# PSUM pools per kind of tile, square sums behind the last blocks, and a source-ordered load queue between the up and down projections

## The chip, the cores and the metric

The kernel runs on one NeuronCore of one Trainium2 chip. The metric is the device time of one execution in microseconds (us); times are medians over executions of the same kernel.

## What is computed

A bidirectional encoder trunk over a sequence of 1024 tokens of width 1024, float32 throughout: an mLSTM layer and a windowed attention layer, each followed by a SwiGLU feed-forward network (FFN) of inner width 2816, and a final RMSNorm. The change touches what surrounds the FFNs.

```python
def rmsnorm(x, w):
    y = x * lax.rsqrt(jnp.mean(x * x, axis=-1, keepdims=True) + EPS)
    return y * w

def swiglu(h, w_in, w_out):
    gu = h @ w_in                                  # 1024 x (2 * 2816)
    gate, up = gu[..., :D_FF], gu[..., D_FF:]
    return (jax.nn.silu(gate) * up) @ w_out

def reference(x, ...):
    for i in range(2):
        hn = rmsnorm(x, norm_mix_w[i])
        x = x + (mlstm_mixer(hn, ...) if i == 0 else window_attn_mixer(hn, ...))
        x = x + swiglu(rmsnorm(x, norm_ffn_w[i]), ffn_w_in[i], ffn_w_out[i])
    return rmsnorm(x, norm_final_w)
```

## The kernel before

**Layout.** Everything is feature-major: x is eight blocks of 128 features by 1024 tokens, `self.x[0..7]`, and each block has two halves of 512 tokens (one PSUM bank holds 128x512 float32). A float32 product is made of three matmuls on parts: each operand is split into a high part (a copy to the narrower type on ScalarE, ACT) and a low part (a subtraction on VectorE, DVE, or on GpSimd, POOL). L200/L201 are the two halves of that split for hidden blocks and for the left operands of the up projection, L187/L188 (ACT, POOL) for the weights of the down projection (`wh`, `wl`). Buffers of 128x1024 come from one shared SBUF pool (`unit`), whether they hold weights as loaded (`raw`), hidden blocks (`hraw`, `hh`, `hl`), blocks of x, or rotary tables (`slab`). Weights are fetched two tiles ahead (`feed`, AHEAD = 2) by SyncE (SP).

**End of a mixer.** `out_pair` multiplies by the output weights block by block; `done` adds each half to x (DVE, L684). In the FFN's mixer, after each pair of blocks (i, i + 4), it also makes the *forms*, the right operands of a Strassen-like product of seven (`norm_forms`: f, f23, f12, f34), squares both blocks (ACT, L291), adds the squares to R (DVE, L292) and stores both blocks to DRAM (`keep_x`, ACT's queue, L243).

**Up projection.** `ffn_up` goes over 22 blocks of 128 hidden features; for each, `seven` (L524) runs seven products into five PSUM accumulators pa, pe, pb, pc, pd, and ACT, DVE and POOL make silu(gate) * up of them. In the first block all five accumulators begin with the first three forms, and the last form comes later. RMSNorm's scale isn't applied to the forms but to the accumulators (`R0`, `R1`): the sums of R over features are 16 matmuls of one column (L357), DVE and POOL make 1/sqrt of them (L345 to L350), two *spreads* (L368, 8 small matmuls each) bring that back to all partitions, and ACT copies them to R (L372). Each finished hidden block goes to DRAM (`hkeep`, L590, ACT's queue).

**Down projection.** `ffn_down` goes over three chunks of hidden blocks (0 to 5, 6 to 13, 14 to 21) and, inside each, over the eight output blocks d; a d of the first chunk is 2 halves of 18 matmuls (L620). Before it, hidden blocks are read back and split (`hidden`), and all of x is read back in 16 halves (`load_x`, L240). Behind each d it adds the product to x (DVE, L647), reads one hidden block of the next chunk, and in the first FFN runs three steps of `rope_tables` (DVE, lines 1107 to 1146), whose positions are loaded by SP (L1109).

**What sets the order.** A compile-time scheduler decides the order of instructions on each engine; each engine then runs its list strictly in order. SP and ACT each have one list in which DMA issues stand with the rest, so an issue that has to wait holds back what follows. DMA completions are counted on eight counters in rotation, and a DMA waits for the one that used its counter before it. `phase` opens the SBUF and the PSUM pool of a stage; in it, tags share the pool, and the next phase's pool takes over banks when the old pool is given back. The banks per tag are mm=2, pn=2, pk=2, mx=2 in the mLSTM phase, mm=3, sc=2, tp=2, mx=1 in the attention phase, and mm=6, mx=2 in the FFN phases.

## Time and profile before

| | us |
|---|---|
| median of 3 executions | 2319.24 (2316.86 to 2319.30) |
| the profiled execution | 2319.65 |
| its span, first to last instruction | 2317.9 |
| tensor engine (PE) busy | 2222.8 (96%) |
| VectorE (DVE) busy | 1403.9 (61%) |
| ScalarE (ACT) busy | 839.3 (36%) |
| GpSimd (POOL) busy | 593.8 (26%) |

The up projections lie at about 510 to 950 and 1605 to 2050 us of the span, each followed by its down projection. In the timelines a row is a start, a duration (or that of several instructions, then with a count) and, in brackets, how long the engine stood before it and what released it. PEclk is the clock that the tensor engine was granted, as a share of 2.4 GHz; 0.5 is its lower level of 1.2 GHz.

### The profile page before, as it was taken

How to read it: one execution, taken by the hardware profiler on the slowest of the kernel's cores; microseconds unless marked ns; L12 is line 12 of the kernel's file. 1: busy time of each engine (PE TensorE's matmuls, PEld its weight loads, DVE VectorE, ACT ScalarE, POOL GpSimd, SP SyncE). 2: the span in 40 equal slices, each digit the busy share in tenths (PEclk: the TensorE clock that was granted, in tenths of full speed). 3: DMA queues.
4: the chain of work that ended last, by engine and by line, in shares of the span. 5: the costliest groups of instructions: out<-in, count | busy, mean ns of one | idle time of the engine just before them, and what ended most of it. 6: DMA issues, size and time to landing. Idle time of an engine off the chain costs nothing.

```text
span 2317.9 us, 28270 instructions
## 1 busy us (share of the span) xinstructions
PE 2222.8 (96%) x10713; PEld 1825.4 (79%) x10713; DVE 1403.9 (61%) x2526; ACT 839.3 (36%) x1544; POOL 593.8 (26%) x398
## 2 busy tenths in 40 slices
PE   7899999989999999999999899898999999999998
PEld 4789898767888888788878777686788888878888
DVE  6355675787666666692224689779866666643112
ACT  4334444343222222321222578665322222232021
POOL 2212213312111111231333455540211111123143
PEclk9999999999999999999999999899999999999999
DMA  3111104222222221632323344503222222263112
GB/s 131 41 37 47 60 24 141 85 108 86 82 82 82 82 82 66 225 127 64 101 73 110 115 144 138 185 16 112 74 81 82 82 82 82 76 242 118 47 54 73
DMA packets 75959, 216.75 MB, mean 94 GB/s; under 512 B 8320, under 2 KB 14976, under 8 KB 75824
## 3 DMA queue, kind: packets, MB, share of 16 engines
q1 hardware_dynamic: 64216, 177.07, 23.6%
q10 hardware_dynamic: 11608, 37.89, 4.1%
q8 instruction: 84, 1.38, 0.2%
q14 instruction: 51, 0.42, 0.1%
HBM read 159.15 MB, written 55.77 MB: 93 GB/s over the span
## 4 chain that ended last, share of the span: by engine, by line
PE 78%; DVE 9%; issue 4%; DMA 3%; POOL 3%; ACT 2%; SPq 0%; POOLq 0%; DVEq 0%; ACTq 0%
PE mm L524 36%; PE mm L620 17%; PE mm L228 14%; PE mm L468 4%; PE pn L212 2%; PE mx L1307 1%; PE tp L1292 1%; PE sc L1263 1%; DMA slab<-bounce 1%; PE pk L212 1%; DMA raw<-in_a_in_dram 1%; DVE slab L1133 1%; DMA slab<-ykeep 1%; DVE e L1268 1%; POOL wl L188 1%
## 5 line engine op out<-in xcount | busy, mean ns | idle before, releaser
L188 POOL TENSOR_TENSOR wl<-raw,wh 128x1024 fp32r<-128x1024 f32 (+2 forms) x96 | 232.8, 2430 | 616.9 <-ACT wh L187 401.7
L620 PE MATMUL mm<-hh,wh 128*128 128x512 f32 (+1 forms) x768 | 289.2, 379 | 7.8 <-ACT wh L187 4.6
L620 PE MATMUL mm<-hh,wl 128*128 128x512 f32 (+1 forms) x768 | 290.4, 378 | 2.1 <-POOL wl L188 2.1
L620 PE MATMUL mm<-hl,wh 128*128 128x512 f32 (+1 forms) x768 | 290.3, 378 | 1.1 <-DVE hl L201 1.1
L571 POOL TENSOR_TENSOR t<-t,R 128x512 f32<-128x512 f32 x44 | 58.6, 1333 | 590.6 <-ACT t L570 590.6
L620 PEld LDWEIGHTS mm<-hh,wh 128*128 128x128 f32 x768 | 145.4, 190 | 37.8 <-ACT wh L187 5.5
L620 PEld LDWEIGHTS mm<-hh,wl 128*128 128x128 f32 x768 | 145.6, 190 | 31.7 <-POOL wl L188 3.3
L620 PEld LDWEIGHTS mm<-hl,wh 128*128 128x128 f32 x768 | 145.6, 190 | 30.8 <-DVE hl L201 2.4
L647 DVE TENSOR_TENSOR x<-x,mm 128x512 f32<-128x512 f32 x80 | 54.7, 685 | 181.6 <-PE mm L620 179.8
L228 PE MATMUL mm<-slab,wh 128*128 128x512 f32 x512 | 152.0, 404 | 5.5 <-ACT wh L187 1.9
L570 ACT ACTIVATE t<-t 128x512 f32<-128x512 f32 x44 | 27.8, 632 | 327.7 <-DVE t L569 327.7
L524 PE MATMUL mm<-f12h,wbl 128*128 128x512 f32 x352 | 138.6, 395 | 0.9 <-DVE wbl L201 0.9
L524 PE MATMUL mm<-f12h,wbh 128*128 128x512 f32 x352 | 138.8, 394 | 0.0
L524 PE MATMUL mm<-f12l,wbh 128*128 128x512 f32 x352 | 138.6, 394 | 0.0
L187 ACT ACTIVATE wh<-raw 128x1024 fp32r<-128x1024 f32 (+3 forms) x106 | 102.0, 969 | 75.0 <-DVE hl L201 57.9
L228 PE MATMUL mm<-hnh,wh 128*128 128x512 f32 x416 | 126.2, 403 | 0.9 <-DVE x L647 0.9
L562 DVE TENSOR_TENSOR t<-mm,t 128x512 f32<-128x512 f32 x44 | 30.4, 692 | 157.0 <-PE mm L524 157.0
L228 PE MATMUL mm<-hnh,wl 128*128 128x512 f32 x416 | 124.4, 400 | 0.4 <-POOL wl L188 0.4
L228 PE MATMUL mm<-hnl,wh 128*128 128x512 f32 x416 | 124.1, 400 | 0.0
L524 PE MATMUL mm<-f,wah 128*128 128x512 f32 x352 | 113.1, 403 | 11.1 <-DVE x L684 11.1
L524 PE MATMUL mm<-f34h,wd 128*128 128x512 f32 x352 | 117.6, 394 | 0.0
L1280 POOL TENSOR_TENSOR e<-e,smd 128x768 f32<-128x768 f32 (+1 forms) x64 | 89.3, 1397 | 101.7 <-DVE smd L1279 62.4
(291 smaller groups left out, 5292.0 us busy)
## 6 DMA issues: line engine op xcount, KB each, us to landing
raw<-in_ffn_in_dram SPq DMA_DIRECT2D x88, 512.0 KB
hkeep<-hs ACTq DMA_DIRECT2D x44, 512.0 KB
hraw<-hkeep SPq DMA_DIRECT2D x44, 512.0 KB
raw<-in_ffn_out_dram SPq DMA_DIRECT2D x32, 512.0 KB
raw<-in_m_in_dram SPq DMA_DIRECT2D x24, 512.0 KB
xkeep<-x ACTq DMA_DIRECT2D x24, 512.0 KB
x<-xkeep SPq DMA_DIRECT2D x48, 256.0 KB
bounce<-slab SPq DMA_DIRECT2D x40, 256.0 KB
```

The lines of the kernel that those rows point to most:

```text
L187: nc.scalar.activation(hi[:, c], r[:, c], AF.Copy)
L188: (nc.vector if fast else nc.gpsimd).tensor_tensor(lo[:, c], r[:, c], hi[:, c].bitcast(F32), op=ALU.subtract)
L212: self.nc.tensor.matmul(out, lhsT=l, rhs=r, start=start and i == 0, stop=stop and i == len(jobs) - 1,)
L228: self.nc.tensor.matmul(st["ps"], lhsT=l, rhs=r, start=j == 0, stop=j == len(jobs) - 1)
L468: self.nc.tensor.matmul(st[c], lhsT=l, rhs=r, start=j == 0 and a == 0, stop=j == 1 and a == len(jobs) - 1)
L524: self.nc.tensor.matmul(ps, lhsT=l, rhs=r, start=start and j == 0, stop=stop and j == len(jobs) - 1, skip_group_check=True,)
L562: V.tensor_tensor(u2, pb, p1, op=ALU.add)
L570: A.activation(g0, g0, AF.Silu)
L571: G.tensor_tensor(g0, g0, R0, op=ALU.mult)
L620: nc.tensor.matmul(po, lhsT=l, rhs=r, start=j == 0, stop=j == len(jobs) - 1)
L647: V.tensor_tensor(x, x, po, op=ALU.add)
L1280: G.tensor_tensor(e[:, j:j + 2, :n], e[:, j:j + 2, :n], d.unsqueeze(2).broadcast_to([P, 2, n]), op=ALU.mult,)
```

## The change

1. `phase` opens one PSUM pool per tag instead of one for all, so that a bank is given back with its own tag's pool; the FFN phases name mx before mm, so mx takes the first two banks and mm the six behind.
2. In `out_pair`, the squares, the adds to R and `keep_x` of blocks 2 and 6 no longer come between the third and fourth forms but behind the fourth, with those of 3 and 7.
3. From the last block of the up projection to the end of chunk 0 of the down projection, SP takes its instructions in source order (`manual_schedule`, closed behind d = 7). The weight split `ahead()` and hidden blocks 0; 1 and 2; 3; 4 are spread over the last up block, and the last `hkeep` store is issued behind the last of their hh splits (`issue_after`).
4. x is read back in full blocks (`fetch_x`, one load of 128x1024 each): two ahead of the loop and block d + 2 behind d.

The diff, cut to its core:

```diff
...
@@ -104,10 +104,12 @@
     @contextmanager
     def phase(self, name, n_t2, banks, spare=False):
         tc = self.tc
-        with tc.tile_pool(name=name, bufs=2) as tmp:
-            with tc.tile_pool(name=name + "p", bufs=2, space=PSUM) as ps:
-                self.tmp, self.n_t2, self.ps, self.banks, self.spare = tmp, n_t2, ps, banks, spare
-                yield
+        with tc.tile_pool(name=name, bufs=2) as tmp, ExitStack() as es:
+            ps = {
+                tag: es.enter_context(tc.tile_pool(name=name + tag, bufs=n, space=PSUM)) for tag, n in banks.items()
+            }
+            self.tmp, self.n_t2, self.ps, self.banks, self.spare = tmp, n_t2, ps, banks, spare
+            yield
 
     def unit(self, dtype=F32, name="slab"):
         return self.sl.tile([P, UNIT], dtype, name=self.nm(name), tag="unit")[:, :S]
@@ -122,7 +124,7 @@
         return self.t([P, HALF], dtype, "t2", self.n_t2)
 
     def bank(self, tag):
-        return self.ps.tile([P, HALF], F32, name=self.nm(tag), tag=tag, bufs=self.banks[tag])
+        return self.ps[tag].tile([P, HALF], F32, name=self.nm(tag), tag=tag, bufs=self.banks[tag])
 
     def setup(self):
         nc, c = self.nc, self.const
@@ -238,6 +240,11 @@
             o = slice(half * HALF, (half + 1) * HALF)
             for d in range(KT):
                 self.nc.sync.dma_start(self.x[d][:, o], src[:, d, o])
+
+    def fetch_x(self, d):
+        if d < KT:
+            self.x.append(self.unit(name="x"))
+            self.nc.sync.dma_start(self.x[d], self.xkeep[:, d])
 
     def keep_x(self, d):
         self.nc.scalar.dma_start(self.xkeep[:, d, :], self.x[d])
@@ -527,14 +534,18 @@
 
     def ffn_up(self, i):
         nc = self.nc
+        self.order = ExitStack()
         V, A, G = nc.vector, nc.scalar, nc.gpsimd
         cur, self.first = self.first, None
         self.hs = {}
         for f in range(NF):
+            if f + 1 == NF:
+                self.order.enter_context(self.tc.manual_schedule(engines={mybir.EngineType.SP}))
             if f + 1 < NF:
                 nxt, todo = self.left()
             else:
-                nxt, todo = None, [self.ahead] + [lambda k=k: self.hidden(i, k) for k in range(3)]
+                nxt, todo = None, [lambda k=k: self.hidden(i, *k) for k in ((0,), (1, 2), (3,), (4,))]
+                self.ahead()
             more = lambda: todo.pop(0)() if todo else None
             hs = self.unit(name="hs")
             R0, R1 = self.Rv(0), self.Rv(1)
@@ -587,14 +598,17 @@
             V.tensor_tensor(u3, pd, u3, op=ALU.add)
             V.tensor_tensor(hs[:, :HALF], g0, u3, op=ALU.mult)
             more()
-            nc.scalar.dma_start(self.hkeep[i][f], hs)
+            with self.tc.issue_after(self.hi.ins) if nxt is None else nullcontext():
+                nc.scalar.dma_start(self.hkeep[i][f], hs)
             cur = nxt
 
-    def hidden(self, i, f):
-        raw = self.unit(name="hraw")
-        self.nc.sync.dma_start(raw, self.hkeep[i][f])
-        self.hs[f] = self.unit(F32R, "hh"), self.unit(F32R, "hl")
-        self.split(*self.hs[f], raw)
+    def hidden(self, i, *fs):
+        for f in fs:
+            raw = self.unit(name="hraw")
+            self.nc.sync.dma_start(raw, self.hkeep[i][f])
+            hi, lo = self.hs[f] = self.unit(F32R, "hh"), self.unit(F32R, "hl")
+            self.hi = self.nc.scalar.activation(hi, raw, AF.Copy)
+            self.nc.vector.tensor_tensor(lo, raw, hi.bitcast(F32), op=ALU.subtract)
 
     def ffn_down(self, i, which, final=False, spill=None, side=()):
         nc = self.nc
@@ -604,7 +618,9 @@
         for f in range(len(hs), FF_CHUNKS[0][1]):
             self.hidden(i, f)
         self.ahead()
-        self.load_x(self.xkeep)
+        self.x = []
+        for d in range(2):
+            self.fetch_x(d)
         for ci, (f0, f1) in enumerate(FF_CHUNKS):
             last = ci == len(FF_CHUNKS) - 1
             if last:
@@ -647,11 +663,15 @@
                     V.tensor_tensor(x, x, po, op=ALU.add)
                     if last:
                         self.norm_add(d, half)
+                if ci == 0:
+                    self.fetch_x(d + 2)
                 if ahead:
                     self.hidden(i, ahead.pop(0))
                 if ci < 2:
                     for _ in range(3):
                         next(side, None)
+                if (ci, d) == (0, KT - 1):
+                    self.order.close()
                 if last and spill is not None:
                     self.keep_x(d)
         self.norm_end()
@@ -689,9 +709,10 @@
                         for f in todo:
                             f()
                     self.norm_forms(i)
-                    for k in (i, i + 4):
-                        self.norm_square_row(k)
-                        self.keep_x(k)
+                    for j in ((0,), (1,), (), (2, 3))[i]:
+                        for k in (j, j + 4):
+                            self.norm_square_row(k)
+                            self.keep_x(k)
 
             return self.product(pairs, done, 6)
 
@@ -1405,12 +1426,12 @@
     def run(self):
         self.setup()
         self.mlstm()
-        with self.phase("f0", 9, dict(mm=6, mx=2), True):
+        with self.phase("f0", 9, dict(mx=2, mm=6), True):
             self.attn_setup()
             self.ffn_up(0)
             self.ffn_down(0, 2, spill=self.xkeep, side=self.rope_tables())
         self.attn()
-        with self.phase("f1", 9, dict(mm=6, mx=2), True):
+        with self.phase("f1", 9, dict(mx=2, mm=6), True):
             self.ffn_up(1)
             self.ffn_down(1, 4, final=True)
 
```

Three places in the listing of instructions show it. On SP, between the up and the down projection of the first FFN, before (the rows begin with the last of the 16 loads of x, which follow hkeep 5, the last hidden block of chunk 0; hkeep 6 is the first of chunk 1):

```order
L240 DMA x_8193<-xkeep 128x512
L168 DMA raw_8229<-in_ffn_out_dram 128x768
L595 DMA hraw_8256<-hkeep_6_75 128x1024
L1109 DMA slab_8266<-in_pos_dram 128x1024
L168 DMA raw_8293<-in_ffn_out_dram 128x768
L595 DMA hraw_8320<-hkeep_7_76 128x1024
L168 DMA raw_8348<-in_ffn_out_dram 128x768
L595 DMA hraw_8375<-hkeep_8_77 128x1024
```

The same place after the change (lines have moved: L595 is now L608, L168 now L170, L1109 now L1130, and L247 is `fetch_x`):

```order
L608 DMA hraw_8197<-hkeep_5_74 128x1024
L247 DMA x_8203<-xkeep 128x1024
L247 DMA x_8205<-xkeep 128x1024
L170 DMA raw_8226<-in_ffn_out_dram 128x768
L247 DMA x_8253<-xkeep 128x1024
L608 DMA hraw_8255<-hkeep_6_75 128x1024
L1128 DMA invf<-in_invf_dram 128x1
L1130 DMA slab_8265<-in_pos_dram 128x1024
L170 DMA raw_8292<-in_ffn_out_dram 128x768
L247 DMA x_8319<-xkeep 128x1024
```

The load of hkeep 6 stood behind all of x, and now stands behind three blocks of it and ahead of the positions.

On ACT, around the last store of the up projection (hkeep 21), before:

```order
L200 ACTIVATE hh_8119<-hraw_8117 128x1024
L570 ACTIVATE t_1391_8109<-t_1391_8109 128x512
L574 ACTIVATE t_1389_8093<-t_1389_8093 128x512
L590 DMA hkeep_21_90<-hs_8033 128x1024
L200 ACTIVATE hh_8142<-hraw_8140 128x1024
L200 ACTIVATE hh_8163<-hraw_8161 128x1024
L200 ACTIVATE hh_8170<-hraw_8168 128x1024
L200 ACTIVATE hh_8176<-hraw_8174 128x1024
L200 ACTIVATE hh_8182<-hraw_8180 128x1024
L187 ACTIVATE wh_8231<-raw_7899 128x768
L200 ACTIVATE hh_8258<-hraw_8256 128x1024
L187 ACTIVATE wh_8295<-raw_8062 128x768
```

and after (L590 is now L602, the hh splits L610, the wh splits L189, the silus L581 and L585):

```order
L610 ACTIVATE hh_8087<-hraw_8085 128x1024
L610 ACTIVATE hh_8142<-hraw_8140 128x1024
L581 ACTIVATE t_1394_8132<-t_1394_8132 128x512
L610 ACTIVATE hh_8148<-hraw_8146 128x1024
L585 ACTIVATE t_1392_8116<-t_1392_8116 128x512
L610 ACTIVATE hh_8171<-hraw_8169 128x1024
L610 ACTIVATE hh_8192<-hraw_8190 128x1024
L602 DMA hkeep_21_90<-hs_8056 128x1024
L610 ACTIVATE hh_8199<-hraw_8197 128x1024
L189 ACTIVATE wh_8228<-raw_7914 128x768
L610 ACTIVATE hh_8257<-hraw_8255 128x1024
```

Five hh splits stood behind the store; now four stand ahead of it and one behind.

On PE, where the mixer's last product ends and the first up projection begins, before:

```order
L228 MATMUL mm_5067<-slab_4656,wh_4937 128x512
L228 MATMUL mm_5067<-slab_4657,wh_4937 128x512
L228 MATMUL mm_5067<-slab_4656,wl_4938 128x512
L524 MATMUL mm_5142<-f_834_4785,wah_4975 128x512 x2
L524 MATMUL mm_5142<-f_834_4785,wal_4976 128x512
L524 MATMUL mm_5142<-f_852_4876,wah_4975 128x512 x2
```

and after (L228 is now L230, L524 now L531):

```order
L230 MATMUL mm_5040<-slab_4665,wl_4947 128x512
L531 MATMUL mm_5157<-f_834_4794,wah_4984 128x512 x2
L531 MATMUL mm_5157<-f_834_4794,wal_4985 128x512
L531 MATMUL mm_5157<-f_852_4885,wah_4984 128x512 x2
L230 MATMUL mm_5054<-slab_4574,wh_4946 128x512 x2
L230 MATMUL mm_5054<-slab_4629,wh_4946 128x512
```

The first five up-projection matmuls now stand ahead of the mixer's last two groups of 12. On ACT, at the first gates of that up projection, before (R from mx is the spread's copy, the t of L551 a copy of the second block's first accumulator):

```order
L372 ACTIVATE R_4721<-mx_5256 128x512
L570 ACT_TABLE_LOAD
L570 ACTIVATE t_933_5269<-t_933_5269 128x512
L551 ACTIVATE t_947_5333<-mm_5320 128x512
L372 ACTIVATE R_4721<-mx_5262 128x512
L574 ACTIVATE t_930_5251<-t_930_5251 128x512
```

and after (L372 is now L379, L551 now L562, L570 and L574 now L581 and L585):

```order
L379 ACTIVATE R_4730<-mx_5271 128x512
L379 ACTIVATE R_4730<-mx_5277 128x512
L581 ACT_TABLE_LOAD
L581 ACTIVATE t_933_5284<-t_933_5284 128x512
L585 ACTIVATE t_930_5266<-t_930_5266 128x512
L562 ACTIVATE t_947_5348<-mm_5335 128x512
```

The second copy of R moved ahead of the table load, and the copy of the accumulator behind both silus.

## Rows read from the trace of the kernel before

**Rows 1.** The top of the page: busy time, share and instructions of each engine.

```profile
PE 2222.8 (96%) x10713; PEld 1825.4 (79%) x10713; DVE 1403.9 (61%) x2526; ACT 839.3 (36%) x1544; POOL 593.8 (26%) x398
```

**Rows 2.** Timeline of PE at the start of up0.

```profile
514.55 1.19 PE L524 MATMUL mm<-f,wah 128*128 128x512 f32 x2 [5.42 <-DVE x L684]
...
546.69 0.39 PE L524 MATMUL mm<-f23h,wah 128*128 128x512 f32 x1
```

**Rows 3.** Stretches of PE: length, busy (instructions), PEclk, DMA share, GB/s.

```profile
513.00:520.00 7.00, 5.45 (x13) 0.52 0.20 77
...
973.00:980.50 7.50, 6.78 (x16) 0.55 0.68 253
...
2069.40:2076.20 6.80, 5.78 (x14) 0.50 0.89 320
```

**Rows 4.** Timeline of PE in down0: the rows that have idle time.

```profile
954.09 0.74 PE L620 MATMUL mm<-hh,wh 128*128 128x512 f32 x2 [1.56 <-ACT hh L200]
955.35 0.50 PE L620 MATMUL mm<-hl,wh 128*128 128x512 f32 x1 [0.52 <-DVE hl L201]
...
973.06 0.50 PE L620 MATMUL mm<-hh,wh 128*128 128x512 f32 x1 [2.66 <-ACT wh L187]
...
975.28 0.80 PE L620 MATMUL mm<-hh,wl 128*128 128x512 f32 x1 [0.66 <-POOL wl L188]
```

**Rows 5.** Timeline of ACT in down0 (ACTq is its issue of a DMA).

```profile
952.61 0.33 ACTq L590 DMA_DIRECT2D hkeep<-hs  x1
952.98 4.85 ACT L200 ACTIVATE hh<-hraw 128x1024 fp32r<-128x1024 f32 x5 [4.50 <-DVE hs L588]
...
971.22 1.06 ACT L200 ACTIVATE hh<-hraw 128x1024 fp32r<-128x1024 f32 x1 [12.66 <-DMA hraw<-hkeep]
```

**Rows 6.** SP from 930 to 1040: two of its waits, and its issue of hraw 6.

```profile
SPq L595 <- DVE hl L201: 27.8, 3, 15.1
SPq L240 <- DMA hkeep<-hs: 13.9, 1, 13.9
...
964.04 0.32 SPq L595 DMA_DIRECT2D hraw<-hkeep  x1
```

**Rows 7.** PE's waits, 1575 to 1650 and 2030 to 2075: total, times, longest.

```profile
PE mm L524 <- DVE x L684: 5.6, 1, 5.6
...
PE mm L620 <- ACT wh L187: 2.0, 1, 2.0
PE mm L620 <- ACT hh L200: 1.6, 1, 1.6
PE mm L620 <- POOL wl L188: 1.5, 1, 1.5
PE mm L620 <- DVE hl L201: 0.5, 1, 0.5
```

**Rows 8.** Stretch 980 to 1000 (PE, PEld, DVE, ACT, POOL, PEclk), and POOL's timeline in it.

```profile
980.00:1000.00 20.00, 20.00 (x87) 16.15 (x87) 19.86 (x19) 3.02 (x4) 5.53 (x3) 0.99 0.15 53
...
987.67 2.97 POOL L188 TENSOR_TENSOR wl<-raw,wh 128x768 fp32r<-128x768 f32 x1 [6.95 <-issue]
994.47 1.85 POOL L188 TENSOR_TENSOR wl<-raw,wh 128x768 fp32r<-128x768 f32 x1 [3.83 <-ACT wh L187]
```

**Rows 9.** Stretch 505 to 530, columns as in rows 8, and DVE's timeline.

```profile
505.00:530.00 25.00, 19.58 (x75) 15.42 (x74) 24.22 (x29) 16.48 (x19) 0.00 (x0) 0.86 0.23 85
...
517.87 2.55 DVE L292 TENSOR_TENSOR R<-R,sq 128x1024 f32<-128x1024 f32 x2
...
532.57 0.16 DVE L345 TENSOR_SCALAR nv<-mx 128x4 f32<-128x4 f32 x1 [1.75 <-PE mx L357]
```

**Rows 10.** Timeline of ACT at the first gates of up0.

```profile
541.12 1.28 ACT L570 ACT_TABLE_LOAD   x1
...
542.95 0.58 ACT L551 ACTIVATE t<-mm 128x512 f32<-128x512 f32 x1
545.73 0.60 ACT L372 ACTIVATE R<-mx 128x512 f32<-128x512 f32 x1 [2.20 <-PE mx L368]
```

More of the change, by code (lines that the diff above doesn't have):

```diff
@@ L1 @@
 import math
-from contextlib import ExitStack, contextmanager
+from contextlib import ExitStack, contextmanager, nullcontext
 from fractions import Fraction
```

## The prediction

> **What bounds the kernel now.** I began with the top of the page: the tensor engine (PE) is busy for 2222.8 us, 96% [rows 1] of a span of 2317.9. So an edit can only pay where PE stands still or is clocked down, some 95 us in all, and an edit that frees another engine pays nothing by itself. Second I listed PE's waits around the four places where the order of instructions differs: the start of the first up projection (up0, near 510 us), its hand-over to the first down projection (down0, near 950), and the same two places of the second FFN (up1 near 1605, down1 near 2050). Third came the granted clock of each stretch, and fourth the engine that PE waits for, in the timelines of ScalarE (ACT), VectorE (DVE) and SyncE (SP).
>
> *Up0.* PE waits 5.42 us, until 514.55, for a DVE add of L684 [rows 2]. That add empties the last PSUM bank of the mixer's pool. The first five L524 groups need data that is ready long before, but their banks come from a new pool, and that opens when the old pool is empty as a whole. Behind the wait the granted clock is 0.52 over 7 us with 5.45 us of PE work [rows 3], which is the lower level, 1.2 GHz; 5.45 x (1 - 0.52) = 2.6 us are lost there.
>
> *Down0.* PE waits 1.56 + 0.52 us for hidden block 1 (hh, hl), then 2.66 us for a weight's high part (wh) and 0.66 for its low part: 5.4 us [rows 4]. Behind the third the clock is 0.55 with 6.78 us of work [rows 3]: 3.0 us lost. The causes stand on two queues. ACT's row at 952.61 is the store of hidden block 21, and the five hh splits stand behind it, 952.98 onwards [rows 5]; the store waits for DVE's product, the splits' data had been in SBUF for longer. On SP the load of the fourth half of x waits 13.9 us for that store to land [rows 6]; behind it stand the other loads of x and then hraw 6, which is issued at 964.04. ACT's split of hraw 6 therefore waits 12.66 us for a transfer until 971.22, and wh, whose raw block is there, stands right behind it [rows 5].
>
> *Up1* shows the wait again, 5.6 us [rows 7]. *Down1* has waits of 2.0, 1.6, 1.5 and 0.5 = 5.6 us [rows 7], and 5.78 us of work at clock 0.50 [rows 3], 2.9 us lost. An idle time of 2.66, 5.42 or 5.6 us was followed by half clock every time; 1.56 and 0.52 close together were not.
>
> **Part 1: SP in source order, store behind the splits, x two blocks at a time.** No arithmetic is added or removed; SP issues 8 full blocks of x in place of 16 halves per FFN. ACT now splits hidden blocks 1 to 4 before the last store and block 5 right behind it, so the 1.56 and the 0.52 go. SP issues hraw 0 to 5, x0, x1, a weight, x2 and hraw 6 before it reaches the load (positions, in down0) that shares a completion counter with the last store; so hraw 6 is issued near 944 (SP reached the x loads at 940 before, and some six issues of 0.7 us follow), not at 964.04, and wh of block d = 2 does not queue behind it: the 2.66 and the 0.66 go, and with them the half clock. Down0: 5.4 + 3.0 = 8.4 us; down1: 5.6 + 2.9 = 8.5 us. What is late next? In down0 the rotary tables (DVE lines L1110 to L1146) follow the position load and fill DVE to 19.86 of 20 us [rows 8]; the down projection's x adds, hl splits and, on GpSimd (POOL), wl splits meet them. One wl split takes 2.97 us beside them and 1.85 without [rows 8]. PE now comes some 5 us sooner to the first weight of the second chunk, which needs a buffer that the rotary work holds. I give back between 0 and 3 us and take 1.0, one wl split's stretch (2.97 - 1.85 = 1.1). So down0 is worth 7.4.
>
> On that stretch the Trainium skill (SBUF — State Buffer, "SBUF: two separate sides") says that GpSimd and a VectorE operation with two SBUF inputs take turns on one shared port pair, the loser waiting for the whole instruction. The two rows agree in direction; by it every wl split of chunk 0 could be delayed by a whole DVE operation, which would be the upper end of the give-back, not another sum.
>
> **Part 2: one PSUM pool per tag, mx first.** In up0, the five accumulators pa to pd now lie in a pool that reuses banks 2 to 7, and the tail of the mixer's phase holds only the mm banks 0 and 1 at that time. Five L524 instructions move ahead of the mixer's last two groups (the listing shows it), and behind them PE goes on: 5.42 us of wait and 2.6 us of half clock are removed there. In up1 the attention phase's mm pool holds banks 0 to 2, so bank 2 still has to be emptied by L684: the 5.6 us wait stays, and its half clock too. Net there 0, with bounds of -1 and +1 for the small waits that change places.
>
> **Part 3: square sums of the last blocks behind the forms.** Here is what up0 is really bound by: the RMS statistics. The sum over squares (R) feeds 16 tiny matmuls, a chain of short DVE and POOL operations, two spreads, and only then the gates of the first block. Before, R is complete near 530.1 and the chain begins at 532.57 [rows 9]; PE resumes with the second block's a12 group at 546.69 [rows 2]. DVE is busy for 24.22 of the 25 us from 505 to 530 [rows 9], so next to nothing on it starts sooner because PE does. The two adds that stood at 517.87 (2.55 us) [rows 9], those of blocks 2 and 6, move behind the last forms to the two of 3 and 7, where a PSUM add (L562, 0.68) and a weight split (1.22) of the next block come among them; that makes R complete some 1.9 to 2.4 us later, near 532.5. Then I followed PE by the listing, with rows' durations: 0.2 to 1.4 us each at five groups that now come before their forms or banks (some 3 in all), some 2 us before the second spread, and then the copy of the second block's pa (L551), for which it needs the bank's value. ACT's order there changes: before, it was R copy, table load (1.28), silu, pa copy at 542.95, and the second R copy at 545.73 [rows 10]; now both R copies stand first, then the table load, two silus and the pa copy. From a second R copy near 542.5: 0.60 for it, 1.28 for the load, 0.6 for a silu (as the copies of that size), 0.2 for DVE's product, 0.6 for silu 2 and 0.58 for the copy give 546.3 for the a12 group. Against 546.69 that is a gain of 0.4, and the 0.44 wait for wbl behind it may go or stay: up0's 8 us are eaten by the chain, not saved. And PE stands for some 5.5 of the 6.5 us before 546.3, with about 1 us of matmuls in it. By the idles above I expect the half clock to come there instead of at 514: + 2.6 by the row of 513 to 520. I take -0.6 + 2.6 = +2.0 for up0; bounds -0.6 (no half clock) and +4 (waits twice as long as worked out).
>
> The table load is one place where a page and a row part: the Trainium skill (ScalarE: Activation LUTs, "What ACT_TABLE_LOAD costs") gives a load of 1283 ns plus a drain of 1380 ns. Here the pa copy started 1.83 us after the load's start with one silu between [rows 10]; a load of 1.28 and a silu of about 0.6 fill that, so the trace bears out the first figure and leaves no room for the second. With the page's drain the pa copy, and with it the whole, would come 1.4 us later: 2307.1, inside the range of the first case below.
>
> **Sum.** 2319.65 (the profiled execution, 0.4 above the median of 2319.24) - 7.4 (down0) - 8.5 (down1) + 2.0 (up0) + 0 (up1) = 2305.75. All other work has the same order on PE; POOL's order doesn't change, and the load of a rotary constant that moves on SP from the start to the positions is one issue (0.3 us) in a queue that stands idle.
>
> **Rivals.**
> 1. *The sum as given*, with up0 between -0.6 and +4 and the give-back in down0 between 0 and 3: 2302 to 2310. Chance 0.63.
> 2. *Up0 pays in full.* If the chain's later start is covered after all (DVE and ACT begin each step as soon as the banks come free, some 5 us sooner), both the 5.42 and the 2.6 stay saved: 2319.65 - 7.4 - 8.5 - 8.0 = 2295.8. For it: PE's wait there is the longest of all. Against it: DVE is full through the whole stretch. Chance 0.10.
> 3. *Half of the down gains is given back.* The wait moves from hraw 6 to a later block, because x2 to x7 now stand between weights and hidden blocks on SP. One more stop of about 2.7 us with its half clock (3.0) in one of the two stages gives 2305.75 + 5.7 = 2311.5; one in each 2317, which is no change. Chance 0.14 and 0.06.
> 4. *Slower: SP's fixed order starves the weights.* Each x(d+2) load needs a free buffer and stands ahead of the next hidden block and weight. SP already waits 15.1 us at once for a buffer that hl holds [rows 6]. One block d of chunk 0 is 36 matmuls, at 20 us for 87 [rows 8] 36 x 0.230 = 8.3 us, and weights are fetched two ahead, so a stop of less than about 16.6 us is hidden. From there each us is PE's: a stop of 25 us costs 8.3 + 3.0 in each stage, 2305.75 + 22.6 = 2328. It decides only if two x loads in a row wait for hl as long as the longest today. Chance 0.05.
> 5. *The pool change does nothing in up0 either* (a bank of the old phase is in the way as in up1): the wait of 5.42 stays, and the chain ends 2 later: the sum differs by 0 to +2, 2306 to 2308; it lies in the range of the first. Chance 0.02.
>
> **How the numbers follow.** The likeliest case gives 2305.75, say 2305.7. From 2297 to 2313 lie the first, the fifth, the single stop of the third and part of the second. A measurement of this kernel tells some 0.2% (4.6 us) from no change, so faster means under 2314.6: cases 1, 2, 5 and the single stop, 0.88 after a little for the unforeseen; the double stop is the same, 0.07; the fourth is slower, 0.05.
>
> **What would show it.** Right: PE's waits in down0 and down1 under 2 us together and no stretch of half clock there; hraw 6 issued near 944 and not after the store's landing; up0 without an L684 wait, a wait for ACT's L551 copy (its line moved by 11) of 3 to 4 us, and the half clock behind it; up1 with its 5.6 us. Wrong: half clock absent from up0 (2303), SP stops over 15 us with raw blocks behind them (case 4), or the first a12 group of up0's second block well before 546, which would mean that the chain is not the bound.

## The result, and the profile after

The changed kernel takes 2302.37 us (median of five executions, 2301.47 to 2303.50) where the kernel before takes 2319.24 (five, 2316.86 to 2320.35): a ratio of 0.9929, with a 95% interval of 0.9918 to 0.9940. The profiled execution took 2302.37 us, with a span of 2300.6. PE is busy for 2216.2 us, 6.6 less than before, although it runs the same matmuls: that is half clock that is gone.

To see where the time went, I took the start of the same matmul, counted along PE's program, in each trace, and subtracted. The marks stand at 499, 593, 936, 1043, 1601, 1741, 2042 and 2093 us of the kernel before, so that each stage has one of the places of the change in it. The table has all kernels of this study, each row from the one profiled execution of its kernel; the first column begins and the last one ends with the span. The experiments are described below. In e8 the marks are moved by the 14 matmuls that it adds in each up projection, whose time is in its row.

| us between marks | to 499 | up0 | up | down0 | attention | up1 | up | down1 | rest |
|---|---|---|---|---|---|---|---|---|---|
| before | 499.0 | 94.0 | 343.1 | 107.1 | 558.0 | 139.9 | 301.1 | 51.1 | 224.8 |
| changed | 497.6 | 95.8 | 342.8 | 99.6 | 558.4 | 138.9 | 301.0 | 41.8 | 224.8 |
| e1_pools | 497.9 | 91.3 | 342.8 | 106.9 | 557.5 | 140.0 | 301.2 | 48.5 | 224.3 |
| e2_squares | 497.5 | 93.1 | 343.3 | 107.6 | 557.7 | 139.2 | 301.1 | 52.1 | 224.7 |
| e3_handover | 498.7 | 93.2 | 343.1 | 99.7 | 556.8 | 140.2 | 301.1 | 41.6 | 224.4 |
| e4_order_halves | 498.9 | 93.1 | 343.1 | 105.5 | 556.1 | 139.2 | 300.8 | 48.2 | 224.2 |
| e5_fetch_only | 498.1 | 93.0 | 343.1 | 103.7 | 560.6 | 139.3 | 301.0 | 44.4 | 224.9 |
| e6_late_gates | 497.9 | 88.2 | 342.5 | 99.7 | 557.4 | 138.3 | 300.9 | 41.7 | 224.8 |
| e7_attn_mm2 | 498.0 | 95.7 | 342.8 | 99.6 | 559.8 | 141.9 | 301.1 | 41.8 | 224.5 |
| e8_filler | 498.6 | 94.5 | 342.6 | 99.6 | 560.3 | 141.9 | 301.5 | 41.8 | 224.6 |
| e9_both | 498.4 | 88.2 | 342.5 | 99.7 | 557.3 | 134.0 | 301.1 | 41.8 | 224.8 |
| e10_rope2 | 496.8 | 88.2 | 342.5 | 98.9 | 560.4 | 134.0 | 300.8 | 41.9 | 224.9 |
| e11_handover_late | 496.8 | 91.2 | 342.9 | 99.6 | 559.1 | 138.0 | 300.6 | 41.7 | 224.8 |
| e12_handover_pools | 499.1 | 91.3 | 342.9 | 99.9 | 557.8 | 139.9 | 300.9 | 41.8 | 224.4 |

The changed kernel gains 7.5 us in down0, 9.3 in down1 and 1.0 in up1, and loses 1.8 in up0. The 1.4 us before the first mark are not of the change: PE's order there is the same in all fourteen kernels, and the stretch takes between 496.8 and 499.1 us in them, with the kernel before near the upper end. The attention stage wanders in the same way, by up to 4.5 us (556.1 in e4, 560.6 in e5). Up0 and up1 scatter less, but they do: kernels in which PE has the same order there differ by 1.0 us (up0 93.0 to 94.0 in the kernel before, e3, e4 and e5; up1 139.2 to 140.2 in the kernel before, e1, e3, e4, e5 and e12). So the 1.0 us in up1 can hardly be told from no change.

**Up0.** This is PE's timeline in the changed kernel, the answer to [rows 2]: the row behind the mixer's last product, where it runs on, then both spreads and the first matmul of the second block's a12 group.

```profile
508.24 0.39 PE L531 MATMUL mm<-f,wal 128*128 128x512 f32 x1
...
537.64 1.13 PE L375 MATMUL mx<-ident,rcol 128*128 128x128 f32 x8 [0.78 <-DVE nv L352]
539.97 2.05 PE L375 MATMUL mx<-ident,rcol 128*128 128x128 f32 x8 [1.21 <-DVE rcol L357]
545.65 0.80 PE L531 MATMUL mm<-f23h,wah 128*128 128x512 f32 x1 [3.63 <-ACT t L562]
```

PE goes from the mixer into the up projection without a stop, runs some 8 us ahead, and stands still at the spreads and then for ACT's copy of the second block's pa. ACT's timeline shows why that copy is late, to be read beside [rows 10]: it stands behind the second R copy, the table load and both silus.

```profile
542.06 0.60 ACT L379 ACTIVATE R<-mx 128x512 f32<-128x512 f32 x1 [2.66 <-PE mx L375]
542.67 1.28 ACT L581 ACT_TABLE_LOAD   x1
543.97 0.63 ACT L581 ACTIVATE t<-t 128x512 f32<-128x512 f32 x1
544.50 0.61 ACT L585 ACTIVATE t<-t 128x512 f32<-128x512 f32 x1
545.02 0.58 ACT L562 ACTIVATE t<-mm 128x512 f32<-128x512 f32 x1
```

**The clock**, stretches with columns as in [rows 8] (PEclk is the last figure but two). The half clock has left the start of up0 and both hand-overs and has come to the a12 group. It sets in before the 3.63 us wait: the second spread's eight matmuls already take 2.05 us, where the first's take 1.13 (rows above).

```profile
545.00:552.00 7.00, 6.35 (x19) 5.04 (x20) 5.76 (x6) 4.07 (x6) 2.18 (x2) 0.64 0.22 84
513.00:520.00 7.00, 7.00 (x30) 5.13 (x29) 7.00 (x10) 4.98 (x6) 0.00 (x0) 1.00 0.18 75
...
960.00:980.00 20.00, 20.00 (x88) 16.17 (x88) 14.09 (x13) 5.40 (x6) 6.44 (x3) 1.00 0.57 222
...
2060.00:2080.00 20.00, 20.00 (x88) 16.19 (x87) 6.54 (x8) 3.38 (x4) 3.73 (x3) 1.00 0.35 106
```

**Down0 and up1.** PE's waits from 940 to 1040 are one row; in down1, from 2020 to 2065, there is none at all. Against [rows 4] and [rows 7] that is 1.3 us instead of 11.

```profile
PE mm L636 <- DVE hl L611: 1.3, 1, 1.3
```

From 1565 to 1640, up1, the wait for the old pool stays, as in [rows 7]:

```profile
PE mm L531 <- DVE x L704: 5.7, 1, 5.7
```

SP, beside [rows 6]: hidden block 6 is issued at 943.99, 20 us sooner, and it is the load of the positions (L1130) that now waits for the last store.

```profile
943.99 0.35 SPq L608 DMA_DIRECT2D hraw<-hkeep  x1
944.38 0.43 SPq L1128 DMA_DIRECT2D invf<-in_invf_dram  x1
955.64 0.33 SPq L1130 DMA_DIRECT2D slab<-in_pos_dram  x1
```

### The profile page after: what moved, and what is told of

Read it like the earlier page. It is cut to its first block, busy times and chain, and to the rows that moved or that the text cites. A ratio compares the mean times of both kernels' runs of the same rounds, so it can differ in the third digit from the quotient of the medians.

```text
span 2300.6 us, 28252 instructions
## 1 busy us (share of the span) xinstructions
PE 2216.2 (96%) x10713; PEld 1822.1 (79%) x10713; DVE 1404.1 (61%) x2526; ACT 837.9 (36%) x1544; POOL 587.5 (26%) x398
## 4 chain that ended last, share of the span: by engine, by line
PE 43%; DVE 4%; DMA 3%; ACT 2%; POOL 2%; issue 1%; SPq 0%; POOLq 0%; ACTq 0%; DVEq 0%
PE mm L531 18%; PE mm L636 18%; PE mm L230 3%; DMA slab<-bounce 1%; DMA raw<-in_a_in_dram 1%; PE sc L1284 1%; PE mx L1328 1%; PE tp L1313 1%; ACT e L1293 1%; DMA slab<-ykeep 1%; DVE smd L1299 1%; DVE e L1289 1%; POOL slab L1191 0%; DVE t L203 0%; POOL e L1301 0%
## 5 line engine op out<-in xcount | busy, mean ns | idle before, releaser
L230 PE MATMUL mm<-slab,wh 128*128 128x512 f32 x512 | 152.9, 406 | 5.4 <-ACT wh L189 1.9
L581 ACT ACTIVATE t<-t 128x512 f32<-128x512 f32 x44 | 27.8, 632 | 327.5 <-DVE t L580 327.5
L531 PE MATMUL mm<-f12l,wbh 128*128 128x512 f32 x352 | 138.6, 394 | 0.0
L531 PE MATMUL mm<-f12h,wbl 128*128 128x512 f32 x352 | 138.4, 394 | 0.0
L531 PE MATMUL mm<-f12h,wbh 128*128 128x512 f32 x352 | 138.2, 394 | 0.0
L189 ACT ACTIVATE wh<-raw 128x1024 fp32r<-128x1024 f32 (+3 forms) x106 | 102.0, 968 | 68.4 <-DVE hl L611 43.5
L230 PE MATMUL mm<-hnh,wh 128*128 128x512 f32 x416 | 126.0, 402 | 0.9 <-DVE x L663 0.9
L230 PE MATMUL mm<-hnh,wl 128*128 128x512 f32 x416 | 123.7, 398 | 0.4 <-POOL wl L190 0.4
L230 PE MATMUL mm<-hnl,wh 128*128 128x512 f32 x416 | 123.2, 397 | 0.0
L531 PE MATMUL mm<-f34h,wd 128*128 128x512 f32 x352 | 117.8, 395 | 0.0
L531 PE MATMUL mm<-f,wah 128*128 128x512 f32 x352 | 111.8, 398 | 5.7 <-DVE x L704 5.7
L230 PEld LDWEIGHTS mm<-slab,wh 128*128 128x128 f32 x512 | 95.3, 192 | 25.2 <-ACT wh L189 2.7
```

The lines of the kernel that those rows point to most:

```text
L189: nc.scalar.activation(hi[:, c], r[:, c], AF.Copy)
L230: self.nc.tensor.matmul(st["ps"], lhsT=l, rhs=r, start=j == 0, stop=j == len(jobs) - 1)
L531: self.nc.tensor.matmul(ps, lhsT=l, rhs=r, start=start and j == 0, stop=stop and j == len(jobs) - 1, skip_group_check=True,)
L581: A.activation(g0, g0, AF.Silu)
```

## Experiments

Parts are numbered as in the prediction: part 1 is the hand-over (points 3 and 4 of the list of changes), part 2 the pools, part 3 the squares. My theory before the first runs was that of the prediction: the gain lies in the hand-overs alone, and up0 is bound by the RMS chain, which eats what the pools save. The rival was that the pool wait is the cost in up0 and that something else takes its place, which could be moved. The kernel before had a median of 2317.14 us beside e1 to e4 (25 executions), 2319.31 beside e5, e6, e7 and e9, 2318.24 beside e8 and e10, and 2318.67 beside e11 and e12; the ratios are to it.

### One part of the change at a time

**e1_pools**: part 2 alone.

```diff
-            with tc.tile_pool(name=name + "p", bufs=2, space=PSUM) as ps:
...
+            ps = {
+                tag: es.enter_context(tc.tile_pool(name=name + tag, bufs=n, space=PSUM)) for tag, n in banks.items()
+            }
...
-        with self.phase("f0", 9, dict(mm=6, mx=2), True):
+        with self.phase("f0", 9, dict(mx=2, mm=6), True):
```

> The kernel before with part 2 alone (one PSUM pool per tag, mx first). Theory, the chain bounds up0: the 5.4 us wait for L684 at the start of up0 goes, but the right operands of the fourth form and the sums of R stand in DVE's order as before, complete near 530; PE waits some 4 to 6 us for the fourth form (L201, L205) between 517 and 528 instead, and the second block's a12 group comes within 1 us of 546.7. Time between 2317 and 2321. Rival, the pool wait itself is the cost: the wait and its half clock are saved whole, 2319.2 - 8 = 2311. The start of up1 keeps its 5.6 us in both.

Measured: 2314.77 us, ratio 0.9988 (0.9979 to 0.9997); up0 takes 91.3 us, 2.7 less. Neither side had it. PE does wait for the fourth form, but only 1.8 us, and its a12 group comes at 542.24, 4.4 us before 546.69 (of which 1.1 lie before the first mark). In this kernel ACT copies pa right behind the second R copy, with one silu ahead of it and not two. The rows are from PE's timeline, then from ACT's.

```profile
542.24 0.50 PE L526 MATMUL mm<-f23h,wah 128*128 128x512 f32 x1 [1.39 <-ACT t L553]
```

```profile
541.12 0.58 ACT L374 ACTIVATE R<-mx 128x512 f32<-128x512 f32 x1
541.60 0.59 ACT L553 ACTIVATE t<-mm 128x512 f32<-128x512 f32 x1
```

Its down1 is 2.6 us shorter, too, with the code unchanged: the wait for wh there is 0.5 us in this trace instead of 2.0. I don't count that to the pools.

**e2_squares**: part 3 alone.

```diff
-                    for k in (i, i + 4):
-                        self.norm_square_row(k)
-                        self.keep_x(k)
+                    for j in ((0,), (1,), (), (2, 3))[i]:
+                        for k in (j, j + 4):
+                            self.norm_square_row(k)
+                            self.keep_x(k)
```

> The kernel before with part 3 alone (squares of blocks 2 and 6 behind the fourth form). Theory, the chain bounds up0 and up1: the wait for L684 and its half clock stay in both; R is complete up to 2 us later; the a12 group comes 0 to 3 us later in up0 and between 1.5 sooner and 1 later in up1. Time 2317.5 to 2322. Rival, an earlier fourth form lets PE run ahead and pays: 2317 or less, with the a12 group of up0 1 to 2 us sooner.

Measured: 2315.37 us, ratio 0.9993 (0.9984 to 1.0002), which cannot be told from no change. The wait for L684 stays (PE's timeline):

```profile
513.05 1.19 PE L524 MATMUL mm<-f,wah 128*128 128x512 f32 x2 [5.41 <-DVE x L684]
```

The a12 group begins at 544.93, 1.8 us sooner, but 1.5 of that lie before the first mark. Up0 takes 93.1 us instead of 94.0 and up1 139.2 instead of 139.9, no further from it than kernels with the same order (93.0 and 139.2). So neither side is decided: the squares alone cost nothing that shows, and that they pay is not shown. With e1 one would expect some 3 us to be gained in up0; in the changed kernel the two parts cost 1.8 there. That had to be explained.

**e3_handover**: part 1 alone (SP in source order, splits ahead of the store, `fetch_x`), all of the diff but its pools and squares.

> The kernel before with part 1 alone (SP in source order, splits ahead of the store, x two blocks at a time). Theory, all of the gain is at the two hand-overs: 7.5 us in down0 and 8.5 in down1, no half clock there, up0 and up1 as before; 2319.2 - 16.0 = 2303.2, within 1.5. Rival, the pools and squares carry part of the gain of the changed kernel: 2306 or more.

Measured: 2300.72 us, ratio 0.9928 (0.9913 to 0.9943); 16.4 us less, down0 99.7 and down1 41.6 us. The whole gain of the change is part 1; the other two parts, as they stand together, add nothing.

**e4_order_halves**: e3 with the old loads of x.

```diff
-        self.x = []
-        for d in range(2):
-            self.fetch_x(d)
+        self.load_x(self.xkeep)
...
-                if ci == 0:
-                    self.fetch_x(d + 2)
```

> Part 1 without the block-wise loads of x: SP in source order and splits ahead of the store, but all 16 halves of x still loaded ahead of hidden block 6. Theory, hidden block 6 behind the loads of x is what holds the weights' high part: the waits for hidden block 1 (2.1 us in each hand-over) go, PE comes that much sooner to the same late load, and waits 4 to 5 us for wh instead of 2 to 2.7, with half clock behind it; 2316 to 2320, as before. Rival, the order of ACT and SP is what pays and the size of the loads does not matter: 2303 to 2305.

Measured: 2314.81 us, ratio 0.9987 (0.9977 to 0.9996). The waits for hidden block 1 are gone, and PE waits longer for the weight, 4.7 us instead of the 3.3 of [rows 4], from 940 to 1045:

```profile
PE mm L627 <- ACT wh L187: 2.7, 1, 2.7
PE mm L627 <- POOL wl L188: 2.0, 2, 1.0
```

SP's timeline has the reason: 16 halves in a row, one of which stands on the last store's landing, and hidden block 6 behind them.

```profile
938.79 20.44 SPq L240 DMA_DIRECT2D x<-xkeep  x16
960.00 0.33 SPq L168 DMA_DIRECT2D raw<-in_ffn_out_dram  x1
960.70 0.78 SPq L601 DMA_DIRECT2D hraw<-hkeep  x1
```

It is issued 3.3 us sooner than in [rows 6], not 20, so most of PE's earlier arrival is spent at the weight, and the gain is 1.6 and 2.9 us.

**e5_fetch_only**: the kernel before with `fetch_x` alone; SP in the scheduler's order, the store ahead of the splits.

> The kernel before with x loaded block by block, two ahead, and nothing else (the scheduler orders SP, the last store stays ahead of the hh splits). Theory, hidden block 6 behind the loads of x is the larger cause: the waits for wh and wl and the half clock go in both hand-overs, the 2.1 us for hidden block 1 stay; about 6.3 and 6.4 us less, of which some 1.6 is given back in the first; ratio to the kernel before 0.994 to 0.996. Rival, the order on SP is needed too, since the third block of x still waits for the last store's landing: ratio 0.998 or more.

Measured: 2309.61 us, ratio 0.9957 (0.9946 to 0.9968); down0 103.7, down1 44.4. That is 3.4 and 6.7 us less, against 4.7 and 6.4 expected. The third block of x still waits for the store, but hidden block 6 stands right behind it, at 953.75 (SP):

```profile
953.34 0.32 SPq L245 DMA_DIRECT2D x<-xkeep  x1
953.75 0.38 SPq L600 DMA_DIRECT2D hraw<-hkeep  x1
```

What is left of the waits is that for hidden block 1 (PE) and, in down0 alone, 1.3 us for a later block's low part, as in the changed kernel. The wait for block 1 brings a half clock of its own in down0, in down1 not (stretches behind it and around it, columns as in [rows 8]):

```profile
952.15 0.73 PE L627 MATMUL mm<-hh,wh 128*128 128x512 f32 x2 [1.56 <-ACT hh L200]
953.41 0.80 PE L627 MATMUL mm<-hl,wh 128*128 128x512 f32 x1 [0.53 <-DVE hl L201]
```

```profile
953.00:960.00 7.00, 6.59 (x22) 5.35 (x23) 4.90 (x5) 5.34 (x7) 2.91 (x1) 0.76 0.80 254
2042.00:2055.00 13.00, 10.90 (x47) 8.22 (x46) 8.94 (x11) 7.38 (x8) 3.64 (x3) 1.00 0.58 217
```

So the loads of x are the larger half of the hand-over, the order of splits and store the smaller: in down1 6.7 (e5) and 2.9 (e4) of the 9.5 of e3. In down0 it is 3.4 and 1.6 of 7.4, so there 2.4 us come only with both.

### What takes the gain in up0

With e1 and e2 the first theory had fallen: the sums of R begin 32.1 to 33.6 us behind the first mark in the kernel before, the changed kernel, e1 and e2, and up0 differs by 4.5 us among them. The new theory: the scheduler puts the copy of the second block's pa behind the gates of the first, and only in the changed kernel behind both silus. PE, which comes early, waits for that copy, and the idle time brings the half clock.

**e6_late_gates**: the changed kernel, with the first block's gates written behind the second block's copy.

```diff
             A.activation(p1, pa, AF.Copy)
+            if f == 1:
+                late()
...
+            def gates(g0=g0, pa=pa, R0=R0, u2=u2, pe=pe, R1=R1):
+                V.tensor_tensor(g0, pa, R0, op=ALU.mult)
+                A.activation(g0, g0, AF.Silu)
...
+            if f:
+                gates()
...
+            if f == 0:
+                def late(gates=gates, hs=hs, u2=u2, c22=c22, g0=g0, u3=u3):
+                    gates()
+                    V.tensor_tensor(hs[:, HALF:], u2, c22, op=ALU.mult)
+                    V.tensor_tensor(hs[:, :HALF], g0, u3, op=ALU.mult)
+                    nc.scalar.dma_start(self.hkeep[i][0], hs)
+
+                cur = nxt
+                continue
```

> The changed kernel, with the gates of the first block of each up projection written behind the second block's copy of pa, so that ACT copies pa ahead of the table load and the silus. Theory, up0 loses its saved time to that copy's place on ACT and to the half clock that the idle time brings: the 3.6 us wait for ACT's copy goes, the waits at the spreads shrink since PE has the a12 group to do between them, no half clock near 546; the a12 group begins 5 to 8 us sooner in up0; ratio to the kernel before 0.989 to 0.991 (the changed kernel: 0.993). Rival, the RMS chain itself is the bound: PE goes on a little and then waits for the banks of the first block (g0, u2) as long as before; ratio 0.993.

Measured: 2294.15 us, ratio 0.9897 (0.9878 to 0.9915); up0 88.2, 7.6 less than the changed kernel. ACT's timeline decides between the theories: the pa copy comes 5.3 us ahead of the first R copy, and the second R copy comes at 545.38, 3.3 us *later* than in the changed kernel.

```profile
534.41 0.60 ACT L562 ACTIVATE t<-mm 128x512 f32<-128x512 f32 x1 [4.49 <-PE mm L531]
539.70 0.60 ACT L379 ACTIVATE R<-mx 128x512 f32<-128x512 f32 x1 [4.70 <-PE mx L375]
...
545.38 0.60 ACT L379 ACTIVATE R<-mx 128x512 f32<-128x512 f32 x1 [3.14 <-PE mx L375]
```

PE, in the stretch from 530 to 555, is at the full clock:

```profile
530.00:555.00 25.00, 23.69 (x118) 19.59 (x119) 21.59 (x41) 8.93 (x12) 8.54 (x6) 1.00 0.22 61
```

A later R with a faster up0: the RMS chain is not the bound, the place of one 0.6 us copy behind the first block's gates is.

**e7_attn_mm2**: the changed kernel with other banks in the attention phase.

```diff
-        with self.phase("a", 6, dict(mm=3, sc=2, tp=2, mx=1)):
+        with self.phase("a", 6, dict(mm=2, sc=2, tp=2, mx=2)):
```

> The changed kernel with two mm and two mx banks in the attention phase instead of three and one, so that the second FFN's mm banks (2 to 7) do not overlap the attention phase's mm banks. Theory: the 5.7 us wait at the start of up1 and its half clock go, but, as in up0, the copy of pa behind two silus gives most of it back: up1 between 1 us faster and 3 slower than in the changed kernel; the attention phase changes by at most 3 us; ratio to the kernel before 0.992 to 0.995. Rival: all is saved in up1, ratio 0.990.

Measured: 2308.72 us, ratio 0.9957 (0.9942 to 0.9971), 6 us slower than the changed kernel. The wait for L704 in up1 is gone, so bank 2 was its cause; PE's longest wait there is now the same as in up0, and the stretch from 1625 to 1650 has a clock of 0.80.

```profile
PE mm L531 <- ACT t L562: 3.6, 1, 3.6
```

```profile
1625.00:1650.00 25.00, 19.37 (x78) 15.43 (x78) 18.74 (x35) 8.21 (x11) 6.59 (x5) 0.80 0.19 64
```

Up1 takes 141.9, 3.0 more than in the changed kernel, as much as I had allowed; the attention stage takes 1.4 more, inside its scatter.

**e9_both**: e6 and e7 together.

> Both edits on the changed kernel: pa of the second block copied ahead of the gates, and two mm banks in the attention phase. Theory: with the copy out of the way the pool wait's removal pays in both FFNs, 5 to 8 us in up0 and as much in up1; ratio to the kernel before 0.986 to 0.989. Rival, the RMS chain or the attention phase with two banks takes it back: 0.991 or more.

Measured: 2292.46 us, ratio 0.9887 (0.9868 to 0.9905), the best of the study together with e10. Up1 takes 134.0, 5.9 less than before and 7.9 less than in e7. The bank edit costs 3.0 us in up1 without the copy's new place and gives 4.3 with it (138.3 to 134.0). PE's stretches, clock 1.00 throughout:

```profile
1595.00:1625.00 30.00, 28.49 (x130) 21.73 (x128) 27.86 (x47) 17.62 (x20) 3.02 (x3) 1.00 0.25 88
1625.00:1650.00 25.00, 23.71 (x107) 19.41 (x108) 21.88 (x29) 9.11 (x12) 6.65 (x5) 1.00 0.40 127
```

**e11_handover_late**: e3 and the later gates, without pools and squares.

> Part 1 of the change and the later gates, without the pools and the moved squares. Theory, the pool per tag is worth its whole 8 us in up0 as soon as the copy of pa does not stand behind the gates, and nothing without it: here the 5.4 us wait for L684 and its half clock stay in up0, and the gates' new place gives at most 2 us per up projection; ratio to the kernel before 0.991 to 0.993. Rival, the later gates alone carry the gain of e6_late_gates: ratio 0.990.

Measured: 2297.01 us, ratio 0.9906 (0.9892 to 0.9919). Up0 takes 91.2 us with the old wait in place, and up1 138.0:

```profile
PE mm L529 <- DVE x L720: 5.4, 1, 5.4
```

Against e3, from which it differs by the gates alone, that is 2.0 and 2.2 us less, about the 2 that I had put as a limit. So the later gates pay something by themselves, too. The pools and squares, which cost 2.6 in up0 without them (e3 to the changed kernel), give 3.0 (91.2 to 88.2) with them.

**e12_handover_pools**: parts 1 and 2 without part 3.

> Parts 1 and 2 of the change without the moved squares (part 3). ACT's order at the first gates is then R copy, table load, silu, R copy, pa copy, silu, with one silu ahead of the copy instead of two. Theory, by e1_pools: up0 is 3 to 4 us faster than in the kernel before instead of 1.7 slower; the a12 group begins near 542 and no half clock follows it; ratio to the kernel before 0.9905 to 0.992. Rival, the squares' place does not matter and up0 stays as in the changed kernel: 0.993.

Measured: 2300.03 us, ratio 0.9916 (0.9903 to 0.9930). Up0 takes 91.3, 4.5 less than the changed kernel, with the copy at one silu's distance as in e1:

```profile
PE mm L531 <- ACT t L562: 1.4, 1, 1.4
```

So the moved squares, which show nothing by themselves, turn the pools' gain of 2.7 into a loss of 1.8, through the order on ACT. The ratios of e12 and of the changed kernel overlap; the stage and the wait do not.

### The half clock and the give-back

**e8_filler**: the changed kernel with useless matmuls in PE's idle time.

```diff
+            if f == 1:
+                junk = self.bank("mx")
+                for _ in range(14):
+                    self.nc.tensor.matmul(junk, lhsT=cur["a11"][0][:, :P], rhs=self.forms[0]["b11"][0], start=True, stop=True, skip_group_check=True)
             self.seven(cur, pa, "a12", "b21", start=False)
```

> The changed kernel with 14 matmuls of 128x512 that nothing needs, put on PE right behind the second spread of each up projection (they write a free bank and their result is not used; the outputs are the same). In up0 they fill the 3.6 us in which PE waits for ACT's copy of pa; in up1, where no such wait is, they add 14 x 0.23 = 3.2 us. Theory, the half clock near 546 comes from the idle time before it: with the time filled it does not come, the a12 group begins at the same place as in the changed kernel (within 0.6 us), and up0 ends 1.5 to 2.2 us sooner in spite of 3.2 us more work; the whole is 1 to 2 us slower than the changed kernel, from up1; ratio to the kernel before 0.993 to 0.995. Rival, the half clock has another cause (its phase, the narrow matmuls of the spreads): half clock stays, up0 does not gain, ratio 0.994 to 0.996 and PEclk near 0.64 in the 7 us from the a12 group.

Measured: 2307.12 us, ratio 0.9950 (0.9934 to 0.9967): 4.8 us above the changed kernel and not 1 to 2, with 3.0 of it in up1, as much as the fillers there, and most of the rest in stretches that scatter (1.9 in attention, 1.0 before the first mark). A ratio of 0.995 fits both sides; the rows have to decide. PE's timeline, then the 7 us of the a12 group:

```profile
541.04 2.05 PE L375 MATMUL mx<-ident,rcol 128*128 128x128 f32 x8 [1.21 <-DVE rcol L357]
542.74 4.19 PE L571 MATMUL mx<-f,wah 128*128 128x512 f32 x14
546.77 0.46 PE L531 MATMUL mm<-f23h,wah 128*128 128x512 f32 x1
```

```profile
545.00:552.00 7.00, 6.63 (x29) 4.92 (x28) 5.41 (x7) 4.69 (x8) 2.54 (x2) 1.00 0.19 75
```

The a12 group starts where it did (546.77, in an execution that is 1.0 us later from before the first mark on; 545.65 in the changed kernel), but at the full clock, and up0 takes 94.5 instead of 95.8 with 3.2 us more work in it. The half clock does come, though, and my theory was wrong in that: the second spread takes 2.05 us here too, and the fillers took 4.0 us and not 3.2. So the clock falls at that spread in both kernels, before the time that the fillers fill; what the idle time does is to keep it down into the a12 group. The spreads alone don't make it fall: in e1 and e12, where they follow each other without a wait of PE, they take 1.05 and 1.13 us. Whether the waits of 0.79 and 1.21 us ahead of them are enough by themselves, no run here parts.

**e10_rope2**: e9 with fewer rotary steps per block in chunk 0.

```diff
-                    for _ in range(3):
+                    for _ in range(3 if ci else 2):
                         next(side, None)
```

> Both edits of e9_both, and two rotary steps per output block in chunk 0 of the first down projection instead of three (three in chunk 1 as before). Theory, the 1.3 us wait for a hidden block's low part at the start of chunk 1 comes from rotary work on DVE and the wl splits of POOL beside it: with less of it there the wait goes, 1.0 to 1.6 us less than e9_both in down0; ratio to the kernel before 0.986 to 0.9885. Rival, the late low part comes from the loads or from ACT: the wait stays, ratio as e9_both (0.9887).

Measured: 2291.93 us, ratio 0.9887 (0.9873 to 0.9902), as e9. Down0 is 0.8 us shorter (98.9; 99.6 to 99.9 in all other kernels with part 1 whole), and the wait is smaller but there (940 to 1060):

```profile
PE mm L654 <- DVE hl L629: 1.0, 1, 1.0
```

Rotary work delays the low part, but less of it removes only a part of the wait; where the rest comes from stays open. A gain of 0.8 us lies under what the whole can show.

## Why the prediction was right, point by point

- **Down0 and down1.** Forecast 7.4 and 8.5 us; measured 7.5 and 9.3, and e3 has both without the rest (7.4 and 9.5). Where the 0.8 us more in down1 come from stays open. The causes held too: e5 shows the loads of x ahead of hidden block 6 (6.7 of 9.5 in down1), e4 the store ahead of the splits (2.9). Hidden block 6 was issued at 943.99, forecast 944. The Trainium skill (TensorE: Matmul & The Clock Gate, "Part 1: The HAM clock gate") says that an idle PE falls to the lower clock; here each hand-over had 5.4 to 5.6 us of waits and lost some 3 more to it, so the clock made up about a third of the gain.
- **The give-back** was forecast at 1.0 us, with the right cause and the wrong carrier: I had named a weight's buffer held by rotary work; PE waits 1.3 us for a hidden block's low part on DVE. The rows, DVE and POOL of the changed kernel, are these; the DVE operation took 3.42 us where it otherwise takes 1.22, beside two wl splits.

```profile
1018.92 3.42 DVE L611 TENSOR_TENSOR hl<-hraw,hh 128x1024 fp32r<-128x1024 f32 x1
```

```profile
1016.03 5.22 POOL L190 TENSOR_TENSOR wl<-raw,wh 128x1024 fp32r<-128x1024 f32 x2 [9.13 <-ACT hh L610]
```

  The Trainium skill's rule on the shared port pair (SBUF — State Buffer, "SBUF: two separate sides") agrees: hl has two inputs in SBUF and ends just behind the splits, at 1022.3 against 1021.3.
- **Up0** was forecast at +2.0 and cost +1.8. The order from the listing held row by row: no L684 wait, a wait for the pa copy of 3 to 4 us (3.63), the a12 group near 546.3 (545.65), half clock behind it (0.64). The size is in part luck. Counted from the first mark, the a12 group comes 0.4 us later than in the kernel before (48.1 and 47.7), where the sum had it 0.4 sooner; from there to the second mark 1.4 us are lost, where the sum had 2.4 (2.6 of half clock, less half of the 0.44 wait for wbl, which went). Two errors of 0.8 and 1.0 us cancel. R's delay, too, was put at 1.9 to 2.4 us and came out as 1.0: the chain begins at 532.18 (DVE, changed kernel) against 532.57 [rows 9], in an execution that is 1.4 us shorter up to the first mark.

```profile
532.18 0.16 DVE L352 TENSOR_SCALAR nv<-mx 128x4 f32<-128x4 f32 x1 [0.81 <-PE mx L364]
```

  What failed is the sentence around it, that up0 is really bound by the RMS statistics. e6 has the second copy of R 3.3 us later and runs up0 7.6 us faster. I had followed one order correctly and then taken it for a law: the copy's place on ACT was in my own sum as "two silus and the pa copy", and it was the bound. The second rival, that up0 pays in full, had been held back for the wrong reason (DVE is full): in e6 DVE is as full, 24.36 of the 25 us from 505 to 530, and up0 pays 5.8 of the 8.0.
- **Up1** was forecast at 0, between -1 and +1, and gave 1.0, at the edge of the bounds and inside the scatter; e2, with the squares alone, gave 0.7. Whether an earlier fourth form pays there stays open. That the 5.6 us wait stays, and why (bank 2), held; e7 removed it.
- **The sum.** 2305.75 forecast, 2302.37 measured: of the 3.4 us, 1.4 are the stretch before the first mark, in which the profiled execution of the kernel before was a long one, 1.0 are up1, 0.8 down1, 0.3 up0 and down0 together, and the rest is 0.1 the other way.
- The rival that SP's fixed order starves the weights did not come: SP's longest wait for hl from 930 to 1030 is 13.5 us, at a load of x, and PE shows nothing of it.

## What to carry to other kernels

A wait that is removed early in a stage is only worth what the next thing in line allows, and that is often a small operation in another engine's queue, not the long chain beside it: look for what stands ahead of it, and change the place in which it is written before giving the gain up for lost. An edit that pays 2.7 us alone and one that shows nothing alone can cost 1.8 together when a scheduler orders the queues; so try them alone and look at the order, not only at the time. Loads that share a queue belong in the order in which they are wanted: 16 loads of x ahead of one hidden block cost 3.4 and 6.7 us here (e5).

## What the hardware showed

Not every idle time of the same size brings the half clock. Waits of 1.56 and 0.52 us in the kernel before [rows 4] did not; the same two in e5, 1.56 and 0.53, did in down0 (PEclk 0.76 behind them) and did not in down1 (1.00). In e1 three waits of 0.54, 0.82 and 0.47 us within 3 us were followed by this stretch:

```profile
520.00:526.00 6.00, 5.41 (x16) 4.03 (x17) 5.57 (x8) 3.32 (x4) 0.00 (x0) 0.72 0.43 149
```

Nor does the same wait always bring the same half clock: behind the 5.4 us wait for L684 in up0, the 7 us from 513 have a PEclk of 0.52 in the kernel before [rows 3] and of 0.76 in e3, e4 and e5, where PE has the same order and as long a wait. That is some 1.2 us of work (5.45 x 0.48 = 2.6 against 5.7 x 0.24 = 1.4 in e3), about up0's scatter. So the price of a wait of about 2 us is the wait, and with some luck not the 1.5 us of half clock behind it (5.41 x 0.28 in the stretch above); a forecast should carry both.

DVE and POOL slow each other [rows 8]: in e10 two rotary operations took 4.57 us beside a wl split, where two of them take 2.48 us with POOL idle in the kernel before. The rows are DVE's in the kernel before and in e10, then POOL's in e10.

```profile
1001.04 2.48 DVE L1133 SCALAR_TENSOR_TENSOR slab<-slab,slab 128x1024 f32<-128x1024 f32 x2
...
1001.66 4.57 DVE L1172 SCALAR_TENSOR_TENSOR slab<-slab,slab 128x1024 f32<-128x1024 f32 x2
```

```profile
1001.91 3.25 POOL L190 TENSOR_TENSOR wl<-raw,wh 128x1024 fp32r<-128x1024 f32 x1 [7.23 <-ACT wh L189]
```
